# A transformer layer in split fp32: twelve instead of eight projection pairs by seven half products, with other step times and longer reckoned transfers

## The chip, the cores and the metric

One NeuronCore of one Trainium2 chip runs one launch of the whole layer. The metric is the device time of the launch in microseconds, median over runs. The engines of the core are PE (matrix products), DVE (VectorE), ACT (ScalarE), POOL (GpSimd) and SP, which here only issues transfers.

## What is computed

One encoder layer on x of 512 tokens by 1024 channels, all in float32 (DFF = 2816):

```
proj = h @ w_in                       # q, k, v of both mixers: 3840 columns
qa, ka, va, qb, kb, vb = split(proj)  # rope_partial on the first 16 of 64 channels of each head's q and k
o_a = windowed_gqa_sink(qa, ka, va, sink)   # 16 heads, 4 kv heads, |i-j| <= 128
o_b = dilated_mixture(qb, kb, vb)           # 3 groups of 4 heads, strides 1, 4, 16
gates = sigmoid(h @ w_gate + b_gate)        # 2 x 1024
mixed = g_a * (o_a @ w_br_a) + g_b * (o_b @ w_br_b)
h = layer_norm(ALPHA * h + mixed @ w_out)
f = (silu(h @ w_ff_gate) * (h @ w_ff_up)) @ w_ff_down
h = layer_norm(ALPHA * h + f)
```

## The kernel before

**Split fp32.** Each fp32 operand is kept as a high part (rounded to the type `fp32r`) and a rest. A product is three matmuls: high by high, high by rest, rest by high. The high part is a copy, on ACT as a rule and on DVE where that is free; the rest is a subtraction on DVE. Splitting the weights is most of the work of both engines.

**Units and pairs.** The weights lie in units of 128 output columns by 1024 rows, as two halves of 512 rows (128 partitions by 512 columns, 256 KB each). A plain unit (`feat_x`) loads two halves, splits both, and runs 8 row blocks x 3 matmuls over all 512 tokens: 24 matmuls of 512 columns. `pair_x(ua, ub)` does two units at once as a two by two block product (two units by two row halves, times two row halves by two token halves) with seven instead of eight half products: the weight blocks are A11, A12, A22 and the sums S1 = A21 + A22, S3 = A11 + A21, S2 = S1 + A11 and S4 = A12 + S2 (up to the signs), the x blocks are B11, B21, B22 and T1 to T4, which the step X (`x_forms`) makes once from x. Each half product is 4 x 3 matmuls over 256 columns, 84 for the pair. `fetch` loads A11, A12, A22 and the first part of S1 and S3 on SP; the second part of S1 and S3 is a transfer on POOL that adds into the block already there (`load_sum`). `form` makes S2 and S4 with one DVE addition each, `sep` splits the seven blocks (the copy on ACT, the subtraction at L399 before), and two DVE operations and four ACT copies put the result together.

**Rotation.** q and k of a plain unit are rotated out of PSUM in `rotate`: four DVE operations over 128 partitions, one of them a stream shuffle that swaps the rotated halves. Tiles that lie in SBUF are rotated together in `turn_rows`: their few rotated rows (16 of each 64) are brought by small transfers on SP into one tile G, shuffled into H, multiplied, added, and brought back. `q_post`, `k_post` then move halves with further SP transfers (L811).

**What sets the order.** Nothing runs in the order of the text. Every `op(...)` is recorded with the engines that can do it, a cost, the tiles it reads and writes and a priority: the time `pr.T` that PE's recorded work has reached, plus an offset (weight work lies 130 us ahead, `LOOK`). `Program.run` then plans the whole kernel: at each moment every free engine takes the ready operation of the lowest priority whose buffers fit the limits (`ws` for blocks as loaded, `whl` for split ones, `gen` for the rest). The outcome is a fixed order on each engine, and on the chip each engine runs its own in that order, waiting for semaphores. For transfers, the planner reckons a landing time from rates and constants (`LATE`, 2.4 or 3.2 us and so on). The words of `ORDER` are the steps that are recorded, in turn:

```
for w in ORDER.split():
    step(w)
```

`VA`, `V0`, `V12` are values; `q1`, `k1`, `Q10`, `K10` and so on are q and k units; `P:a,b` is a pair of units; `g` is a gate unit (its number counts up by itself); `R` turns the tiles gathered since the last R; `A0` to `A3` are the attention of mixer A by key head, four query blocks each, `B0` to `B3` mixer B by head slot; `O` fetches a block of A's output; `L` sets limits. After them come the branch products, the output product, the first norm, and the feed-forward stage, which also uses seven half products, and the second norm.

Of the kernel before, what the change touches and what calls it, by code (L numbers as in the profile page):

```python
# [15 lines left out]
P = 128  # L16
# [36 lines left out]
SPARE, SPARE2 = 12, 12  # L53
# [10 lines left out]
LATE = 2.4  # L64
OAP = (-88.0, -88.0, -88.0, -88.0)
# [29 lines left out]
BY_DMA = ()  # L95
AWAY = range(8, 16)
N_WSA, N_WHLA = 8, 16
# [36 lines left out]
class Program:  # L134
# [67 lines left out]
    def run(self):  # L202
# [26 lines left out]
        while n_left:  # L229
# [11 lines left out]
            while progress:  # L241
                progress = False
                for e in engines:
# [27 lines left out]
                    if e == SP:  # L271
                        end = now + (0.62 if 14 < now < SLOW else 0.47)
                        moved = max(moved, now + 0.9) + (1.5 if now < 9.5 else RATE if 90 < now < 165 else RATE2 if 285 < now < 325 else 1.0 if now < SLOW else 0.92) * cost
                        o.done = moved + (LATE if 95 < now < 150 else 2.4 if 14 < now < SLOW else 0.87)
                    elif o.moves:
                        end = now + cost
                        moved = max(moved, end + 0.3) + (1.0 if 14 < now < SLOW else 0.92) * o.moves
                        o.done = moved + (0.87 if e == ACT else 6.2 if ACC < now < 420 else 3.2 if 14 < now < SLOW else 2.2)
                    else:
                        end = now + cost  # L280
                        o.done = end
# [50 lines left out]
def hybrid_layer(ctx: ExitStack, tc: tile.TileContext, wpack, xT, xtok, sink, bgate,  # L332
# [10 lines left out]
                  "unit": UNITS, "oa": N_OA, "st": 4, "x4": 4, "wf": N_WF})  # L343
# [250 lines left out]
    def pair_x(ua, ub):  # L594
# [12 lines left out]
        def form(key, of, x, y):  # L607
            tt(lambda: W[of].t, lambda: W[x].t, lambda: W[y].t, ALU.add, [W[x], W[y]], [W[of]], S, -LOOK)
# [93 lines left out]
    def turn_rows(tiles):  # L702
# [6 lines left out]
        for i, R in enumerate(tiles):  # L709
# [5 lines left out]
        op([(DVE, dve(S, extra=0.03))], lambda e: nc.vector.stream_shuffle(h_(), g(), SHUF2), reads=gs, writes=[H], prio=EV)  # L715
# [3 lines left out]
           reads=[H, *[(s_, i) for i in range(4)]], writes=[H], prio=EV)  # L719
# [156 lines left out]
    def turned_values(u, nt, turn_by=0, done=None):  # L876
# [3 lines left out]
        for i in range(2):  # L880
            ps = done
# [18 lines left out]
        for b in range(NR):  # L900
# [6 lines left out]
            op([(PE, 0.18)], turn, reads=[*src, ident], writes=[pb])  # L907
# [46 lines left out]


# [11 lines left out]
    def turned_probs(srcs, toks):  # L967
# [7 lines left out]
        op([(PE, 0.36)], go, reads=[*toks, ident], writes=[pb])  # L975
# [6 lines left out]
    def turned_pairs(srcs, toks):  # L982
# [7 lines left out]
        op([(PE, 0.36)], go, reads=[*toks, ident], writes=[pb])  # L990
# [60 lines left out]
    def unit_b(hs, q, k, v0, v1, v2):  # L1051
# [99 lines left out]
        dil = []  # L1151
        for half in range(2):
# [5 lines left out]
            def pv(e, half=half, xs=xs, od=od):  # L1158
# [7 lines left out]
                y for vs in (v1, v2) for t in vs[2 * half:2 * half + 2] for y in vtok(t)], writes=[od])  # L1166
            t = slot(F32, "att")
            dil.append(t)
            part = lambda od=od: od.t.rearrange("p (r i a) -> p r a i", r=2, a=2)
# [32 lines left out]
        t = slot(F32, "att")  # L1202
        op(cp_alts(S, True), lambda e: copy(e, t.t[0:64], o.t[64:128]), reads=[o], writes=[t])
        a = 64 * (hs % 2)
# [27 lines left out]
    def gate(f, ps=None):  # L1232
        if ps is None:
# [6 lines left out]
           reads=[ps, bg], writes=[t], prio=EV)  # L1240

# [25 lines left out]
    ka = k_near(psk, 4)  # L1267
    qa = q_near(psq, 4, (0, 0))
# [43 lines left out]
    def units_of(w):  # L1312
# [8 lines left out]
        if w[0] == "q":  # L1321
            return U_QA + i, lambda t: qa.extend(q_post(t, 4, ((i // 2) % 2,) * 2))
        if w[0] == "k":
            return U_KA + i, lambda t: ka.extend(k_post(t, 4))
# [4 lines left out]
    def step(w):  # L1329
# [4 lines left out]
        elif w[:2] == "P:":  # L1334
            both = [units_of(x) for x in w[2:].split(",")]
            for (u, f), t in zip(both, pair_x(*[u for u, _ in both])):
# [7 lines left out]
        elif w == "R":  # L1344
            tiles = [t for t, _ in env["turn"]]
            turn_rows(tiles)
# [8 lines left out]
        elif w[0] == "q":  # L1355
            i = int(w[1])
            kv = (i // 2) % 2
            qa.extend(dense_q(U_QA + i, 4, (kv, kv)))
        elif w == "k1":
            ka.extend(dense_k(U_KA + 1, 4))  # L1360
        elif w[0] == "A":
            g = int(w[1])
            for b in range(NR):
                unit_a(g, b, qa[4 * g:4 * g + 4], ka[g], env["va"])
# [4 lines left out]
        elif w[0] in "QK":  # L1369
            pair, g = int(w[1]), int(w[2])  # L1370
            u, f = units_of(w)
            env["turn"].append((in_sbuf(u), f))
        elif w == "V0":
            env["v0"] = turned_values(U_V0, 8, 1)
        elif w == "V12":
# [9 lines left out]
    for w in ORDER.split():  # L1385
# [660 lines left out]
```

## Time and profile before

| what | value |
|---|---|
| median of 3 runs | 727.95 us (727.42 to 728.01) |
| span of the profiled execution, first to last instruction | 725.8 us |
| median run less that span | 2.15 us |
| instructions | 14412 |
| bytes moved by DMA | 140.30 MB, mean 193 GB/s |
| PE, DVE, ACT, POOL busy | 99%, 90%, 65%, 18% of the span |
| mean granted clock of PE | 0.996 |

The profile is of one execution. It gives that execution's span and no time of the whole launch; the timed runs, which are launches, lie 1.6 to 2.2 us above the span. Busy shares of PE overstate its work, since matmuls are pipelined; the list of waits and the distance between starts say more. In a row of waits, "A <- B: 1.2, 1, 1.2" reads: A's engine stood idle before A until B ended, 1.2 us in total, once, 1.2 us at most.

### The profile page before, as it was taken

The page shows a single profiled execution, that of the slowest core. Times are in us where ns is not written, and L with a number is a line of the kernel's source. Part 1 is how long each engine was busy: PE and PEld are TensorE (multiplying, and loading weights), DVE is VectorE, ACT ScalarE, POOL GpSimd, SP SyncE. Part 2 cuts the span into 40 slices and gives each one's busy share as a digit, 9 for nine tenths or more (in the row PEclk, how much of TensorE's full clock was granted, in tenths as well). Part 3 has the DMA queues.
Part 4 walks back from the last instruction along what each step waited for, and adds up shares of the span by engine and source line. Part 5 has one row for each costly group of instructions (what it writes and reads, how often), then busy time and mean ns, then how long its engine had stood idle before and what let it go on. Part 6 is the DMA issues. An engine that isn't in the chain of part 4 may idle for free.

```text
span 725.8 us, 14412 instructions
## 1 busy us (share of the span) xinstructions
PE 717.3 (99%) x4767; PEld 666.2 (92%) x4767; DVE 655.6 (90%) x1408; ACT 471.4 (65%) x1077; POOL 134.0 (18%) x297
## 2 busy tenths in 40 slices
PE   9999999999999999999999999999999999999995
PEld 7889999989988888988888999999999999999985
DVE  6999999889997898898967898899999999899987
ACT  5757798868778665666534666756666566666821
POOL 0021211111100731450020021111112211212000
PEclk9999999999999999999999999999999999999998
DMA  8978788856577689965681499676888888979302
GB/s 256 309 155 202 191 213 246 211 135 172 170 192 185 160 228 253 309 217 185 216 209 44 116 267 228 154 199 155 200 254 212 193 215 225 258 184 200 97 30 87
DMA packets 88010, 140.30 MB, mean 193 GB/s; under 512 B 11136, under 2 KB 24064, under 8 KB 87936
## 3 DMA queue, kind: packets, MB, share of 16 engines
q1 hardware_dynamic: 74336, 114.87, 51.7%
q0 software_dynamic: 13328, 24.39, 20.5%
q8 instruction: 37, 0.61, 0.3%
q14 instruction: 37, 0.30, 0.1%
q10 hardware_dynamic: 272, 0.13, 0.1%
HBM read 114.97 MB, written 7.60 MB: 169 GB/s over the span
## 4 chain that ended last, share of the span: by engine, by line
PE 99%; DVE 1%; DVEq 0%; issue 0%
PE ps L1692 10%; PE ps L1691 9%; PE ps L1690 9%; PE ps L523 9%; PE ps L524 9%; PE ps L525 9%; PE ps L1901 4%; PE ps L1903 4%; PE ps L1902 4%; PE ps L641 3%; PE ps L640 3%; PE ps L639 3%; PE ps L973 3%; PE ps L1480 3%; PE ps L1481 3%; PE ps L1482 3%
## 5 line engine op out<-in xcount | busy, mean ns | idle before, releaser
L373 ACT ACTIVATE sl<-sl 128x512 fp32r<-128x512 f32 (+3 forms) x419 | 230.8, 583 | 59.7 <-DVE sl L544 31.1
L544 DVE TENSOR_TENSOR sl<-sl,sl 128x512 fp32r<-128x512 f32 (+3 forms) x378 | 222.4, 621 | 5.1 <-ACT sl L373 3.4
L373 ACT ACTIVATE sl<-ps 128x256 f32<-128x256 f32 (+5 forms) x209 | 88.7, 445 | 91.6 <-PE ps L1692 56.8
L387 POOL DMA_DIRECT2D sl<-wpack x60 | 53.1, 885 | 342.9 <-DMA sl<-wpack 118.2
L1691 PE MATMUL ps<-sl,sl 128*128 128x256 f32 x352 | 96.8, 275 | 0.0
L1692 PE MATMUL ps<-sl,sl 128*128 128x256 f32 x352 | 96.8, 275 | 0.0
L1690 PE MATMUL ps<-sl,sl 128*128 128x256 f32 x352 | 96.8, 275 | 0.0
L523 PE MATMUL ps<-x,sl 128*128 128x512 f32 (+1 forms) x241 | 93.9, 389 | 0.0
L525 PE MATMUL ps<-x,sl 128*128 128x512 f32 (+1 forms) x241 | 91.4, 379 | 0.0
L524 PE MATMUL ps<-x,sl 128*128 128x512 f32 (+1 forms) x209 | 79.5, 380 | 0.0
L1690 PE MATMUL ps<-x,sl 128*128 128x256 f32 x264 | 72.6, 275 | 0.0
L1691 PE MATMUL ps<-x,sl 128*128 128x256 f32 x264 | 72.6, 275 | 0.0
L1692 PE MATMUL ps<-x,sl 128*128 128x256 f32 x264 | 72.6, 275 | 0.0
L1691 PEld LDWEIGHTS ps<-sl,sl 128*128 128x128 f32 x352 | 67.6, 192 | 0.1
L1690 PEld LDWEIGHTS ps<-sl,sl 128*128 128x128 f32 x352 | 67.6, 192 | 0.1
L1692 PEld LDWEIGHTS ps<-sl,sl 128*128 128x128 f32 x352 | 67.6, 192 | 0.0
L399 DVE TENSOR_TENSOR sl<-sl,sl 128x512 fp32r<-128x512 f32 x94 | 62.8, 682 | 1.8 <-ACT sl L373 1.3
L525 PEld LDWEIGHTS ps<-x,sl 128*128 128x128 f32 x241 | 45.9, 190 | 6.5
L1690 PEld LDWEIGHTS ps<-x,sl 128*128 128x128 f32 x264 | 50.6, 192 | 0.4
L1691 PEld LDWEIGHTS ps<-x,sl 128*128 128x128 f32 x264 | 50.6, 192 | 0.4
L523 PEld LDWEIGHTS ps<-x,sl 128*128 128x128 f32 x241 | 46.0, 191 | 5.4 <-ACT sl L373 0.3
L1692 PEld LDWEIGHTS ps<-x,sl 128*128 128x128 f32 x264 | 50.7, 192 | 0.0
(172 smaller groups left out, 1851.0 us busy)
## 6 DMA issues: line engine op xcount, KB each, us to landing
sl<-wpack SPq DMA_DIRECT2D x249, 256.0 KB, 3.9
sl<-wpack POOLq DMA_DIRECT2D x60, 256.0 KB, 5.3
sl<-sl SPq DMA_DIRECT2D x110, 128.0 KB, 3.1
wf<-wpack SPq DMA_DIRECT2D x51, 256.0 KB, 5.2
wf<-wpack POOLq DMA_DIRECT2D x24, 256.0 KB, 6.2
oa<-sl SPq DMA_DIRECT2D x32, 128.0 KB, 3.6
sl<-sl SPq DMA_DIRECT2D x68, 32.0 KB, 2.6
sl<-oa SPq DMA_DIRECT2D x8, 256.0 KB, 5.1
```

The lines of the kernel that those rows point to most:

```text
L373: nc.scalar.activation(dst, src, AF.Copy)
L387: op([(POOL, 1.0)], lambda e: nc.gpsimd.dma_start(b.t, src2, accum_op=ALU.add), reads=[b], writes=[b], prio=prio, moves=1.65)
L399: op([(DVE, dve(S))], lambda e: nc.vector.tensor_tensor(l.t, src.t, f32(h.t), op=ALU.subtract), reads=[src, h], writes=[l], prio=prio, abs ...
L523: mm(o, a, x0, start=(k == 0 and begins), stop=False, skip_group_check=split)
L524: mm(o, a, x1, start=False, stop=False, skip_group_check=split)
L525: mm(o, b, x0, start=False, stop=(k == nk - 1), skip_group_check=split)
L544: op([(DVE, dve(w))], lambda e: nc.vector.tensor_tensor(dst(), x(), y(), op=o), reads=reads, writes=writes, prio=prio)
L1690: mm(o, wh, pairs(bh[k]()), start=(first and k == 0), stop=False, skip_group_check=True)
L1691: mm(o, wh, pairs(bl[k]()), start=False, stop=False, skip_group_check=True)
L1692: mm(o, wl, pairs(bh[k]()), start=False, stop=(k == 3), skip_group_check=True)
L1901: mm(ps.t, x0, pairs(w[0].t), start=(first and m == 0), stop=False, skip_group_check=True)
L1902: mm(ps.t, x0, pairs(w[1].t), start=False, stop=False, skip_group_check=True)
```

## The change

The table of steps is new. Twelve pairs stand in it instead of eight (the words P and D), and single gates are spread between the last attention steps instead of eight at the end. A number behind `@` shifts the priority of everything that the step records by so many us (negative: earlier). `D:` is a pair whose S2 and S4 are made by transfers on POOL that add one SBUF block into another, and `r` is a turn whose shuffle is made by eight-row transfers on SP instead of a DVE shuffle.

```diff
-VA q1 A0 q2 q3 g X P:k1,q4 R A1 P:q5,g P:q6,q7 R A2 P:g,g A3 P:g,g L P:Q00,K00 R V12 P:Q01,K01 R P:Q02,K02 R V0 B0 Q10 K10 R Q11 K11 R B1 O O Q12 K12 R O O B2 B3 O O O O g8
+q1@-471 X@-159 VA A0@-92 q2@-21 P:q3,g@-28 R@-36 D:k1,q4@-16 R@89 P:q5,Q01@-152 D:q6,q7@-32 r@680 D:g,g P:g,Q00@-10 L P:g,K00@-42 A1@-39
+R@180 V12@-5 P:g,K01@-30 R@22 P:Q02,K02@-15 R@-10 A2@-71 A3@-67 V0@36 P:K10,Q10@-17 B0@-44 O@-1217 O@-237 R@-587 K11@-20 B1@-33 P:Q12,Q11@-22
...
-SPARE, SPARE2 = 12, 12
+SPARE, SPARE2 = (10, 12)
+LONG = 1.3
-FORMS = -60.0
-VAL = -100.0
-OA_AFTER = (0, 0, 0, 0, 0, 0, 0, 0)
+FORMS = -165.0
+VAL = -130.0
+OA_AFTER = (0, 0, 0, 0, 0, 1, 1, 0)
-N_WSA, N_WHLA = 8, 16
+N_WSA, N_WHLA = (8, 18)
...
 (Program.run: the reckoned landing of SP's and of other transfers)
-                        o.done = moved + (LATE if 95 < now < 150 else 2.4 if 14 < now < SLOW else 0.87)
+                        o.done = moved + (LONG if now < 380 else 1.0) * (LATE if 95 < now < 150 else 2.4 if 14 < now < SLOW else 0.87)
...
 (pair_x, form)
+            if by_dma:
+                a, b = W[of], W[x if y == of else y]
+                op([(POOL, 1.0)], lambda e: nc.gpsimd.dma_start(a.t, b.t, accum_op=ALU.add), reads=[a, b], writes=[a],
+                   prio=-LOOK, moves=1.65)
+                W[key] = a
+                return
...
 (turn_rows)
+        if by_dma:
+            hs_ = []
+            for i, R in enumerate(tiles):
+                for h in range(2):
+                    for z in range(2):
+                        hs_.append((H, 4 * i + 2 * h + z))
+                        op([(SP, 0.1)], lambda e, R=R, i=i, h=h, z=z: nc.sync.dma_start(
+                            H.t[32 * i + 16 * h + 8 * z:32 * i + 16 * h + 8 * z + 8], R.t[64 * h + 8 - 8 * z:64 * h + 16 - 8 * z]),
+                           reads=[(R, 1), (R, 2)], writes=[hs_[-1]], prio=EV)
+        else:
+            op([(DVE, dve(S, extra=0.03))], lambda e: nc.vector.stream_shuffle(h_(), g(), SHUF2), reads=gs, writes=[H], prio=EV)
...
 (gate: plain gates of branch B are stored to DRAM and read back later, as those of pairs were)
+        if f in AWAY:
+            put_away(f)
...
 (the planner's costs of transposes on PE)
-        op([(PE, 0.36)], go, reads=[*toks, ident], writes=[pb])
+        op([(PE, 0.436)], go, reads=[*toks, ident], writes=[pb])
...
 (steps)
+        w, _, later = w.partition("@")
+        pr.T += float(later or 0)
         step(w)
+        pr.T -= float(later or 0)
```

The new file also holds code that no word of the table reaches (values by half products, values out of a pair, mixture sums by transfers); q and k tiles are now kept by their unit's number instead of being appended, since units no longer come in sequence. Line numbers are higher by some 4 to 200: a pair's matmuls, L639 to L641 before, are L649 to L651 after; its split at L399 is L403; the DVE helper L544 is L548; the load L381 is L385 and the addition on POOL L387 is L391.

Over the whole program, by the built order: matmuls over 512 columns 1711 before and 1519 after, over 256 columns 2672 and 3008; full tensor operations on DVE 633 and 651, half ones with a scalar 71 and 75, casts of 512 columns 24 and 13, half casts (two shapes of 256 columns) 1 and 8, shuffles 13 and 11; POOL transfers 93 and 107; SP transfers of 256 KB 342 and 352, of 16 rows 72 and 76, of 8 rows 0 and 20.

PE, behind the first five units and one plain unit (names: `ps` is a PSUM tile, `x` holds x split, `sl` a split weight or values). Before, another plain unit (ps116) and, in its middle, the transposes of the values of A:

```order
L525 MATMUL ps116_519<-x47_94,sl80_394 128x512
L905 MATMUL ps121_550<-ident_65,sl99_450 128x128
L905 MATMUL ps121_550<-ident_65,sl119_535 128x128
L905 MATMUL ps122_553<-ident_65,sl99_450 128x128
L905 MATMUL ps122_553<-ident_65,sl119_535 128x128
L523 MATMUL ps116_519<-x442_242,sl82_402 128x512
```

After, behind the same five units and one plain unit (ps94), the first pair begins (256 columns, first product A11 by B11):

```order
L527 MATMUL ps94_451<-x444_245,sl67_336 128x512
L528 MATMUL ps94_451<-x446_253,sl67_336 128x512
L529 MATMUL ps94_451<-x444_245,sl68_337 128x512
L649 MATMUL ps109_509<-x48_98,sl70_345 128x256
L650 MATMUL ps109_509<-x412_105,sl70_345 128x256
L651 MATMUL ps109_509<-x48_98,sl71_346 128x256
```

A plain unit and the values' transposes have moved behind the pair.

POOL, from the first blocks of attention A0 on (COPY is the sink's column for the softmax of one head; L387, L391 add a loaded block; L614 adds one SBUF block into another). Before:

```order
L1020 COPY sl144_627<-nsink_66 128x1
L1020 COPY sl145_630<-nsink_66 128x1
L387 DMA sl152_663<-wpack 128x512
L387 DMA sl173_747<-wpack 128x512
L387 DMA sl201_881<-wpack 128x512
L387 DMA sl211_953<-wpack 128x512
L1020 COPY sl243_1086<-nsink_66 128x1
```

After:

```order
L1198 COPY sl182_858<-nsink_66 128x1
L614 DMA sl138_659<-sl145_685 128x512
L391 DMA sl174_830<-wpack 128x512
L614 DMA sl153_727<-sl161_756 128x512
L1198 COPY sl206_975<-nsink_66 128x1
L1198 COPY sl207_979<-nsink_66 128x1
L1198 COPY sl208_981<-nsink_66 128x1
L614 DMA sl146_688<-sl138_659 128x512
L1198 COPY sl213_996<-nsink_66 128x1
L614 DMA sl164_773<-sl153_727 128x512
```

The S2 and S4 additions of two D pairs (sl138 into sl146, sl153 into sl164) now stand between the copies of A0's second block.

SP, around the first packed turn of more than one tile (L381, L385 load a block; L712, L722 bring rows into G; L732 brings eight rows into H; L1046 stores attention output). Before:

```order
L381 DMA sl211_953<-wpack 128x512
L712 DMA sl214_959<-sl195_835 16x512 x2
L381 DMA sl222_993<-wpack 128x512
L712 DMA sl214_959<-sl206_907 16x512 x2
L381 DMA sl234_1063<-wpack 128x512
L1046 DMA oa236_1071<-sl235_1066 64x4x128
```

After:

```order
L722 DMA sl142_678<-sl128_611 16x512
L385 DMA sl161_756<-wpack 128x512
L722 DMA sl142_678<-sl128_611 16x512
L385 DMA sl164_773<-wpack 128x512
L732 DMA sl169_786<-sl115_532 8x512 x4
L732 DMA sl169_786<-sl128_611 8x512 x2
L385 DMA sl174_830<-wpack 128x512
L732 DMA sl169_786<-sl128_611 8x512 x2
```

The rows for G and H of two tiles now stand among the block loads of the two D pairs (sl161, sl164, sl174).

More of the change, by code (lines that the diff above doesn't have):

```diff
@@ L277, in run @@
                         moved = max(moved, end + 0.3) + (1.0 if 14 < now < SLOW else 0.92) * o.moves
-                        o.done = moved + (0.87 if e == ACT else 6.2 if ACC < now < 420 else 3.2 if 14 < now < SLOW else 2.2)
+                        o.done = moved + (LONG if now < 380 else 1.0) * (0.87 if e == ACT else 6.2 if ACC < now < 420 else 3.2 if 14 < now < SLOW else 2.2)
                     else:
@@ L873, in scores, with turned_values @@
         return go, [(qt, "h"), (qt, "l"), (kt, "h"), (kt, "d"), (kl, "h"), (kl, "d")]
-    def turned_values(u, nt, turn_by=0, done=None):
+    def turned_values(u, nt, turn_by=0, done=None, made=None):
         src = []
@@ L1151, in unit_b @@
         dil = []
+        add_up = hs in SUM_BY_DMA
+        E = [slot(F32, "att"), slot(F32, "att")] if add_up else []
         for half in range(2):
```

203 lines of the change are left out of this document (182 added, 21 removed).

## The prediction

> **What bounds the kernel now.** I read the busy shares first, then who waited for whom, then the busy time by stretch, then the end of the chain that ended last, and last single rows for the price of each instruction.
>
> ```profile
> PE 717.3 (99%) x4767; PEld 666.2 (92%) x4767; DVE 655.6 (90%) x1408; ACT 471.4 (65%) x1077; POOL 134.0 (18%) x297
> ```
>
> The list of waits on PE over the whole run has one entry:
>
> ```profile
> PE ps L459 <- DVE eps L510: 1.2, 1, 1.2
> ```
>
> So the matrix engine waits 1.2 us at the start and then never again. The same by stretch (columns: PE busy, weight loads, DVE, ACT, POOL, granted clock, DMA share, GB/s), and the first and last row of the chain at its end:
>
> ```profile
> 0.00:340.00 340.00, 338.81 (x2109) 309.56 (x2110) 304.43 (x751) 247.60 (x603) 75.09 (x229) 1.00 0.77 210
> 340.00:420.00 80.00, 80.00 (x431) 71.19 (x430) 67.67 (x116) 41.51 (x83) 7.76 (x9) 1.00 0.56 150
> 420.00:700.00 280.00, 280.00 (x2147) 269.57 (x2147) 264.28 (x509) 178.65 (x385) 51.17 (x59) 1.00 0.78 195
> ```
> ```profile
> 718.26 0.23 PE ps L1482
> ...
> 722.15 0.40 DVE sl L1543
> ```
>
> PE is busy for all of 340:700 at full clock, and for all but 1.2 us before. A share of "busy" alone would prove little, since matmuls overlap; but with no wait in the list and one matmul's start on the heels of the next (rows below), PE's own work sets the end at 718.5, and 7.3 us of vector work and store follow. A time saved must therefore come out of PE's sum, and a loss must come as a wait on PE that does not exist today. The second engine is DVE: 304.4 of 340 in the stretch that the change touches, and early on nearly all of it:
>
> ```profile
> 20.00:60.00 40.00, 40.00 (x195) 35.11 (x194) 39.46 (x82) 23.98 (x47) 6.33 (x12) 1.00 0.80 220
> 60.00:110.00 50.00, 50.00 (x428) 49.36 (x427) 47.78 (x104) 44.11 (x106) 10.21 (x18) 1.00 0.81 203
> ```
>
> **The change, PE.** Four more pairs are done by seven half products. Two plain units are 2 x 8 x 3 = 48 matmuls over 512 columns; a pair is 7 x 4 x 3 = 84 over 256. By the built order the counts go from 1711 to 1519 (512 columns) and from 2672 to 3008 (256); transposes and everything else on PE keep their counts, so the change does what it says. The price of one is the distance between starts, not the "mean ns" of a group, which contains the pipeline. Of 28 rows over 512 columns, and of 110 rows over 256, the first and the last:
>
> ```profile
> 46.15 0.38 PE L524 MATMUL ps<-x,sl 128*128 128x512 f32 x1
> ...
> 51.98 0.38 PE L524 MATMUL ps<-x,sl 128*128 128x512 f32 x1
> ```
> ```profile
> 419.81 0.28 PE L1691 MATMUL ps<-x,sl 128*128 128x256 f32 x1
> ...
> 431.98 0.28 PE L1692 MATMUL ps<-sl,sl 128*128 128x256 f32 x1
> ```
>
> (51.98 - 46.15) / 27 = 0.2159 us and (431.98 - 419.81) / 109 = 0.1117 us. The change removes 192 x 0.2159 = 41.45 and adds 336 x 0.1117 = 37.53: PE's work falls by 3.92 us, 0.98 per pair.
>
> The Trainium skill, page "TensorE: Matmul & The Clock Gate", section "Wait — 56ns, not 53.3ns?", puts the step at columns / 2.4 GHz plus about 2.5 ns. It fits the long matmuls here (0.2158 against 0.2159) and not the short ones (0.1092 against 0.1117); by it the saving would be 192 x 0.2158 - 336 x 0.1092 = 4.74 us, an estimate from that page. The measured step decides, so I keep 3.92.
>
> **DVE and ACT.** A plain unit needs two splits into a high part (ACT) and a rest (DVE); a pair needs seven, two sums that form S2 and S4, and two sums at the end. Prices, again by distance of starts where rows follow each other:
>
> ```profile
> 28.31 3.69 DVE L399 TENSOR_TENSOR sl<-sl,sl 128x512 fp32r<-128x512 f32 x6
> 24.15 0.42 DVE L570 SCALAR_TENSOR_TENSOR sl<-sl 128x256 f32<-128x256 f32 x1
> 24.49 0.41 DVE L544 TENSOR_TENSOR sl<-sl,sl 128x256 f32<-128x256 f32 x1
> L375 DVE CAST sl<-sl 128x512 fp32r<-128x512 f32 x14 | 5.8, 420 | 0.7 <-DMA sl<-sl 0.6
> L375 DVE CAST sl<-sl 128x256 fp32r<-128x256 f32 x1 | 0.3, 294 | 0.0
> L715 DVE STREAM_SHUFFLE sl<-sl 64x512 f32<-64x512 f32 x7 | 5.1, 732 | 0.0
> ```
>
> Six in 3.69 us is 0.60 each (3.69 less one tail of 0.08), the half size 0.34, a cast 0.34 and half a cast 0.21 (less the same 0.08), a shuffle 0.65. Counts by the order: +18 full tensor operations (24 for the four pairs, less 6 that the D pairs give to DMA), +4 half ones, -11 casts, +7 half casts, -2 shuffles: 10.8 + 1.4 - 3.7 + 1.5 - 1.3 = +8.7 us. In 0:340, which becomes some 336, DVE then has 313 us of work: 93% against 90%. ACT gains 18 full and 18 half activations, at most
>
> ```profile
> L373 ACT ACTIVATE sl<-sl 128x512 fp32r<-128x512 f32 x337 | 200.7, 622 | 51.9 <-DVE sl L544 30.0 <-DVE sl L747 7.2 <-DVE sl L570 2.7
> L647 ACT ACTIVATE sl<-ps 128x256 f32<-128x256 f32 x32 | 12.0, 375 | 3.7 <-PE ps L641 3.6
> ```
>
> 18 x 0.62 + 18 x 0.38 = 18 us on 248 of 340: no limit. On the path that sets the end I cost DVE and ACT at nothing, since PE's stream covers them; the cover is thin before 110 us, where DVE has 0.54 + 2.22 = 2.76 us free of 90. That is the first rival.
>
> **Transfers.** Each pair loads five blocks on SP and adds two on POOL where two units load four on SP; the three D pairs put two more additions each on POOL, from SBUF to SBUF. That is +14 on POOL. SP gains 34 rows: 4 blocks, 3 gates stored and 3 read back, 20 pieces of 16 KB that replace two shuffles, 4 small turn pieces.
>
> ```profile
> sl<-wpack SPq DMA_DIRECT2D x249, 256.0 KB, 3.9
> sl<-wpack POOLq DMA_DIRECT2D x60, 256.0 KB, 5.3
> sl<-sl SPq DMA_DIRECT2D x110, 128.0 KB, 3.1
> sl<-sl SPq DMA_DIRECT2D x68, 32.0 KB, 2.6
> sl<-oa POOLq DMA_DIRECT2D x8, 256.0 KB, 7.5
> q1 hardware_dynamic: 74336, 114.87, 51.7%
> q0 software_dynamic: 13328, 24.39, 20.5%
> 82.41 1.20 SPq L723 DMA_DIRECT2D sl<-sl  x2
> ```
>
> By queue, POOL's 24.39 MB take 0.84% of the span per MB and SP's 0.45%: 14 x 0.26 MB and 10 x 0.26 MB add about 3.1% + 1.2% of 726 us, 31 us, which over the first 340 lifts the share from 0.77 to about 0.86. There is room. SP's queue gets 34 x 0.6 = 20 us more of issue; what stands behind the small pieces there are weight blocks for products that PE reaches later. An addition from SBUF to SBUF is not in this trace: from below 3.1 us (SBUF to SBUF, half the size, on SP), from above 7.5 (POOL, addition of a block just written); I take 5.3, the row of the same size, queue and operation. It lies beside PE's other work unless the chain in the second rival comes late; bounds on the path: 0 to what is priced there. Not a gain, since nothing waits for the DVE sums today.
>
> **Order.** The first pair now starts right after the first plain unit, the first scores of attention later; the longer reckoned transfers move users of a block later or its load earlier and add no instruction. The feed-forward stage keeps its instructions. Where a place in the order costs PE nothing before, I found none in the new order that must cost: the gaps that the softmax leaves between scores and their transposes, and between transposes and the product with the values, are filled with about as many matmuls as before.
>
> **Sum.** 3.92 us less on PE, nothing added on the path. The profiled span of 725.8 would be 721.9; the median run lies 2.15 above the span (727.95), which is launch and end and stays. Forecast: 727.95 - 3.92 = 724.0.
>
> **Rivals.**
> First, DVE binds early. By the order, PE has done 1.8 pairs where it had just begun its first (57 us of PE work), and 5.1 instead of 4.0 at 107. A pair costs DVE 10 x 0.60 + 0.34 = 6.3 us against 2.4 for two plain units, 3.9 more (2.7 for a D pair). At 107 that is 2.7 to 4.3 us more work against 2.76 us free: up to 1.5 us late; at 57, 1.8 x 2.7 to 3.9 = 4.9 to 7.0, less 2.4 for the four operations of a rotation that moves into the packed turn, against 0.54 free: up to 4.1 late if nothing of it could be done ahead. Against it: attention work that filled DVE there now comes later. In the middle some 2.3 us of waits: 726.3.
>
> Second, the other side: the chain of a D pair. S1 is loaded (3.9), added to (5.3), added into A11 for S2 and that into A12 for S4 (5.3 to 7.5 each): 19.8 to 24.2 us before S4 can be split, where DVE's sums give 3.9 + 5.3 + 1.2 = 10.4. PE eats a pair in 84 x 0.1117 = 9.4. On POOL the addition for S4 stands behind the one for S2 and ahead of copies that the softmax needs, so a late one holds both. If a D pair is late by 1.3 us three times over, the saving is gone; from 1.8 us each it is slower by over 0.2% (3 x 1.8 - 3.92 = +1.5); at 3 us each 727.95 - 3.92 + 9 = 733.0. For it: POOL stops at an addition until the load before it has landed,
>
> ```profile
> POOL sl L387 <- DMA sl<-wpack: 43.7, 6, 32.8
> ```
>
> six times in 20:340; without the idle start (32.8) five times 2.2 us. Against it: PE was held up by none of these, and D products come a pair or more behind their loads in the order.
>
> The Trainium skill, page "TensorE: Matmul & The Clock Gate", section "HAM oscillation — how this bites in real kernels", adds that PE idle for over about 3.4 us comes back at half clock. No stretch here shows it before the end (1.00 throughout), as PE never idles; it would make a long wait dearer by up to about 1.7 us, an estimate from that page's window.
>
> Third, the short matmuls run closer to that page's step than in the row above: 723.2. Little speaks for it, all rows give 0.1117.
>
> **Numbers.** 0.2% of 728 us, 1.46 us, is about what a measurement here can tell from no change. Forecast, PE stays full within a microsecond: 0.63. DVE early (726.3, half of it within 0.2% of before): 0.22. D chain: 0.08, nearly all slower. Short step: 0.03. Other small waits: 0.04, mostly with part of the gain left. Faster 0.80, same 0.13, slower 0.07. Range: 723.2 (the third rival) to 727.4 (the first rival beyond its middle).
>
> **What would show it.** Right: PE's list of waits still has only the entry at the start, PE ends near 714.5, 336 more short and 192 fewer long matmuls at the same steps, DVE near 664 us busy, DMA share in 0:340 near 0.86, the tail 7.3 us. Wrong: a wait of PE on DVE's splits between 35 and 110 us (first rival), or on splits behind the POOL additions with SBUF source between 60 and 150 (second), or a clock under 1.00 after one of them.

## The result, and the profile after

| kernel | median | runs | ratio to before (95% interval) |
|---|---|---|---|
| before | 727.98 us | 727.42 to 728.41 (4) | 1 |
| after | 734.82 us | 733.65 to 737.8 (4) | 1.0099 (1.0074 to 1.0124) |

Forecast were 724.0 us in a range of 723.2 to 727.4, and a slower kernel at 0.07. The change costs 1%; the forecast missed by 10.8 us. Disturbed runs are left out below, one of four of the first e1 and two of four in e11, which e16 repeats.

The busy shares after, first line of the page:

```profile
PE 717.6 (98%) x4911; PEld 668.4 (91%) x4911; DVE 663.0 (91%) x1418; ACT 483.8 (66%) x1109; POOL 150.6 (21%) x311
```

PE has 144 matmuls more, as counted, and DVE 663 us, near the 664 that were forecast. But the profiled span is 732.2 us instead of 725.8, and the list of waits on PE (total, times, longest) is no longer one entry:

```profile
PE ps L1342 <- DVE sl L1176: 3.1, 1, 3.1
PE ps L1218 <- DVE sl L1156: 1.5, 2, 1.2
PE ps L463 <- DVE eps L514: 1.2, 1, 1.2
PE ps L527 <- ACT sl L377: 0.8, 1, 0.8
PE ps L649 <- ACT sl L657: 0.5, 1, 0.5
```

5.9 us of waits are new. Delays too short for the list count as well. I added up over all rows of PE how much farther the next start lies than the price of the row (0.2159 us for 512 columns, 0.1117 for 256, for other shapes their median distance before). After has 10.4 us more of this than before: 0.8 at 80 to 100, 2.1 at 140 to 160, 0.7 at 260 to 280, 6.0 at 280 to 300, 0.4 behind 400, the rest in small amounts. The spans say the same: 732.2 - 725.8 + 3.9 of saved work = 10.3.

To compare kernels below, I call loss what the median lies above before's median on the same chip, plus the 3.9 us of work that twelve pairs save (nothing for eight): 10.8 us for after (734.82 - 727.98 + 3.92).

The stretches of the prediction, after (PE, weight loads, DVE, ACT, POOL, clock, DMA share, GB/s):

```profile
0.00:340.00 340.00, 332.78 (x2224) 306.43 (x2225) 306.52 (x752) 258.07 (x630) 91.35 (x243) 0.99 0.84 225
340.00:420.00 80.00, 79.83 (x402) 70.07 (x401) 66.08 (x113) 40.69 (x81) 6.99 (x8) 1.00 0.58 161
420.00:700.00 280.00, 280.00 (x2176) 270.38 (x2175) 265.92 (x512) 180.58 (x390) 52.30 (x60) 1.00 0.78 199
```

Nearly all that PE loses lies ahead of 340. The same view in finer stretches, before and then after:

```profile
260.00:280.00 20.00, 20.00 (x117) 18.10 (x116) 17.28 (x44) 13.56 (x30) 3.47 (x4) 1.00 0.92 214
280.00:300.00 20.00, 20.00 (x110) 17.83 (x109) 17.27 (x49) 9.71 (x27) 4.07 (x8) 1.00 1.02 288
```
```profile
260.00:280.00 20.00, 19.89 (x125) 17.76 (x124) 18.41 (x55) 15.69 (x42) 9.67 (x36) 1.00 0.83 208
280.00:300.00 20.00, 16.10 (x89) 13.80 (x88) 14.61 (x42) 14.21 (x38) 8.35 (x24) 0.93 1.00 293
```

At 280:300 PE and DVE lose busy time, while the DMA share is at 1.00. It was at 1.02 before, too, and PE did not wait. (A share can pass 1, so it counts packets that overlap, and 1.00 alone does not prove that the engines are full.) What SP issues there after (start, length, line, count; L877 and L832 are moves of 128 KB inside SBUF, L385 loads of weight blocks):

```profile
265.57 7.27 SPq L877 DMA_DIRECT2D sl<-sl  x8
272.95 5.02 SPq L832 DMA_DIRECT2D sl<-sl  x8
278.07 5.22 SPq L877 DMA_DIRECT2D sl<-sl  x8
...
283.97 1.85 SPq L385 DMA_DIRECT2D sl<-wpack  x4
...
289.34 4.89 SPq L385 DMA_DIRECT2D sl<-wpack  x6
```

For 18 us SP issues no weight block, then many. But before had such pauses too, 16 us up to 278.48 and 12 us up to 294.09 (L856 are moves, L381 loads):

```profile
266.46 8.87 SPq L856 DMA_DIRECT2D sl<-sl  x8
...
278.48 1.77 SPq L381 DMA_DIRECT2D sl<-wpack  x4
...
294.09 5.91 SPq L381 DMA_DIRECT2D sl<-wpack  x9
```

What differs is whether somebody stands waiting for the blocks. ACT's waits for weight blocks in 20:340, before and then after:

```profile
ACT sl L373 <- DMA sl<-wpack: 0.7, 1, 0.7
```
```profile
ACT sl L377 <- DMA sl<-wpack: 8.4, 6, 2.8
```

In after, 5.1 of the 8.4 us lie in 280:298. DVE waits there for ACT's copies; below it, the chain up to PE's wait:

```profile
DVE sl L403 <- ACT sl L377: 3.6, 2, 2.5
```
```profile
286.88 6.96 DMA sl<-wpack
...
293.86 0.03 ACT sl L377
...
295.55 0.28 ACT sl L377
...
295.86 0.42 DVE sl L379
296.28 0.34 DVE sl L1176
```

A block on its way for 6.96 us holds ACT's copy up to 293.86. ACT runs its list in order, and the copies of the turned probabilities (295.55) stand behind that one; DVE makes the rest of these (L1176), and PE waits 3.1 us for it. The wait of 1.2 us that ends at 155.35 has the same form: a move of 128 KB, on its way for 5.76 us, holds DVE (L825), and the split that PE needs (L1156) stands behind it. Then PE comes back at half clock, seen in the distance of its starts:

```profile
293.26 0.38 PE L529 MATMUL ps<-x,sl 128*128 128x512 f32 x1
296.76 1.85 PE L1342 MATMUL ps<-sl,sl 128*128 128x256 f32 x8 [3.12 <-DVE sl L1176]
298.40 0.63 PE L527 MATMUL ps<-x,sl 128*128 128x512 f32 x1
298.83 0.63 PE L528 MATMUL ps<-x,sl 128*128 128x512 f32 x1
...
300.52 0.38 PE L529 MATMUL ps<-x,sl 128*128 128x512 f32 x1
300.74 0.38 PE L527 MATMUL ps<-x,sl 128*128 128x512 f32 x1
```

0.43 us from start to start up to 300.5, then 0.22. The record of the granted clock has 0.5 for 3.41 us there: 1.7 us more, which are part of the 6.0.

### The profile page after: what moved, and what is told of

It is laid out like the page before. It is cut to its first block, busy times and chain, and to the rows that moved or that the text cites. A ratio compares the mean times of both kernels' runs of the same rounds, so it can differ in the third digit from the quotient of the medians.

```text
span 732.2 us, 14826 instructions
## 1 busy us (share of the span) xinstructions
PE 717.6 (98%) x4911; PEld 668.4 (91%) x4911; DVE 663.0 (91%) x1418; ACT 483.8 (66%) x1109; POOL 150.6 (21%) x311
## 4 chain that ended last, share of the span: by engine, by line
PE 89%; DVE 4%; DMA 3%; SPq 1%; issue 1%; ACT 1%; DVEq 0%
PE ps L1895 9%; PE ps L1896 9%; PE ps L1894 9%; PE ps L527 6%; PE ps L528 6%; PE ps L529 6%; PE ps L649 4%; PE ps L650 4%; PE ps L651 4%; PE ps L2105 4%; PE ps L2106 4%; PE ps L2107 4%; PE ps L1686 3%; PE ps L1684 3%; PE ps L1685 3%; PE ps L1151 2%
## 5 line engine op out<-in xcount | busy, mean ns | idle before, releaser
L377 ACT ACTIVATE sl<-sl 128x512 fp32r<-128x512 f32 (+3 forms) x437 | 242.0, 586 | 69.9 <-DVE sl L548 41.6
L548 DVE TENSOR_TENSOR sl<-sl,sl 128x512 fp32r<-128x512 f32 (+3 forms) x408 | 240.4, 626 | 2.5 <-ACT sl L377 1.6
L391 POOL DMA_DIRECT2D sl<-wpack x68 | 59.9, 881 | 357.8 <-DMA sl<-wpack 161.5
L377 ACT ACTIVATE sl<-ps 128x256 f32<-128x256 f32 (+5 forms) x206 | 85.7, 438 | 70.8 <-PE ps L1896 52.9
L1895 PE MATMUL ps<-sl,sl 128*128 128x256 f32 x352 | 96.8, 275 | 0.0
L1896 PE MATMUL ps<-sl,sl 128*128 128x256 f32 x352 | 96.8, 275 | 0.0
L1894 PE MATMUL ps<-sl,sl 128*128 128x256 f32 x352 | 96.8, 275 | 0.0
L527 PE MATMUL ps<-x,sl 128*128 128x512 f32 (+1 forms) x177 | 69.5, 393 | 0.8 <-ACT sl L377 0.8
L529 PE MATMUL ps<-x,sl 128*128 128x512 f32 (+1 forms) x177 | 67.5, 382 | 0.0
L403 DVE TENSOR_TENSOR sl<-sl,sl 128x512 fp32r<-128x512 f32 x78 | 52.5, 682 | 5.2 <-ACT sl L377 4.0
L528 PE MATMUL ps<-x,sl 128*128 128x512 f32 (+1 forms) x145 | 55.6, 384 | 0.0
L548 DVE TENSOR_TENSOR sl<-sl,ps 128x512 f32<-128x512 f32 (+1 forms) x71 | 46.5, 659 | 8.2 <-PE ps L2107 5.4
L649 PE MATMUL ps<-sl,sl 128*128 128x256 f32 x192 | 53.5, 278 | 0.0
L650 PE MATMUL ps<-sl,sl 128*128 128x256 f32 x192 | 52.8, 275 | 0.0
L651 PE MATMUL ps<-sl,sl 128*128 128x256 f32 x192 | 52.8, 275 | 0.0
L1895 PEld LDWEIGHTS ps<-x,sl 128*128 128x128 f32 x264 | 50.6, 192 | 0.4
```

The lines of the kernel that those rows point to most:

```text
L377: nc.scalar.activation(dst, src, AF.Copy)
L391: op([(POOL, 1.0)], lambda e: nc.gpsimd.dma_start(b.t, src2, accum_op=ALU.add), reads=[b], writes=[b], prio=prio, moves=1.65)
L527: mm(o, a, x0, start=(k == 0 and begins), stop=False, skip_group_check=split)
L528: mm(o, a, x1, start=False, stop=False, skip_group_check=split)
L529: mm(o, b, x0, start=False, stop=(k == nk - 1), skip_group_check=split)
L548: op([(DVE, dve(w))], lambda e: nc.vector.tensor_tensor(dst(), x(), y(), op=o), reads=reads, writes=writes, prio=prio)
```

## The experiments

Eighteen runs; "after" in them means the changed kernel. Unless said, its planned order is kept on every engine, so that only the edit differs; e6 and e10 to e16 are planned anew.

**First idea: SP's queue (theory 1).** SP was to be relieved of moves, on POOL's queue instead.

```diff
-op([(SP, 0.4)], lambda e, t=t, z=z, a=a, d=d: nc.sync.dma_start(     # k_pairs, L877
+op([(SP, 0.4)], lambda e, t=t, z=z, a=a, d=d: nc.gpsimd.dma_start(
```

> Changed kernel, same planned order, but the moves of L877 (k_pairs, 128 KB each) are issued by POOL's queue instead of SP's; bytes, tiles and users are the same. Theory 1 (SP issues its transfers one after the other, 0.62 to 0.9 us each, and the weight loads behind 26 small moves at 265.5 to 284.0 come too late): sixteen of these 26 leave the queue, the loads at 284 to 288 are issued some 10 us earlier, the wait PE ps L1342 <- DVE sl L1176 of 3.1 us and the slow clock behind it go, about 5 to 6 us: 728 to 730 us. Theory 2 (the additions of the D pairs on POOL) and theory 3 (the 8-row pieces of the turned rows): no change, 734 to 736. Theory 5 (the DMA engines are full there, share 1.00, and the landing is late whoever issues): no change, 734 to 736. If POOL is late instead, its additions are (5.7 us each): then slower than 736.

Measured 736.32 us, ratio 1.0105 (1.0087 to 1.0123): no gain. The chain up to PE's wait:

```profile
282.43 12.49 DMA sl<-wpack
...
297.37 0.34 DVE sl L1176
```

SP issued the four blocks from 278.55 instead of 283.97 on, and the block that the chain hangs on at 282.43 instead of 286.88. Yet it was 12.49 us on its way, and PE waited 3.2 us at the same place. With L832 moved as well:

> As e1_pairs_pool, and the moves of L832 (q_post, k_post) are issued by POOL too: 110 moves of 128 KB leave SP's queue, about 70 us of its issue. Theory 1: the loss at 80 to 100, 140 to 160 and 260 to 300 goes (9 to 10 us), less what comes back because POOL issues a move later than SP did: 725 to 729 us. Theory 5 (full DMA engines): 734 to 736. Theories 2 and 3: 734 to 736.

736.9 us, 1.0115 (1.0081 to 1.0149). Here the edit brings a wait of its own: POOL's additions and its small softmax copies now stand in one list with moves (`272.45 9.87 DMA sl<-oa` in the chain), so the run does not tell the theories apart. In the first one the landing of the block does. The Trainium skill, page "DMA: Bandwidth & Descriptors", section "Issuing engines are not separate DMA queues", says that transfers of all issuing engines share the same 16 DMA engines, and that another issuer saves only the time of issuing. The 12.49 us agree.

**The two new forms of the change (theories 2 and 3).**

```diff
-nc.gpsimd.dma_start(a.t, b.t, accum_op=ALU.add)          # form, D pairs
+nc.vector.tensor_tensor(a.t, a.t, b.t, op=ALU.add)
```

> Changed kernel, same planned order, but the six additions from tile to tile of the D pairs (POOL, 256 KB, 5.7 us each) are done by VectorE (six adds of 128x512, about 0.62 us each, 3.7 us of VectorE). Theory 2 (the chain of transfers of the D pairs delays their products): 728 to 731 us. Theory 1 (SP's queue): these additions stand on POOL, SP is as before, so 734 to 737, the larger value where VectorE's 3.7 us more stand in the stretch in which PE waits for it. Theory 5: 1.5 MB less of moving at 60 to 260, but none at 260 to 300: at most 1 us gain.

735.47 us, 1.0097 (1.008 to 1.0115), the same wait, 4.3 us long: the additions of the D pairs are not the cause.

```diff
-nc.sync.dma_start(H.t[... 8 rows ...], R.t[...])   # 20 of them, L732
+nc.vector.stream_shuffle(h_(), g(), SHUF2)          # at the place of the last of each turn
```

> Changed kernel, same planned order, but the 20 transfers of 8 rows (L732) are left away and VectorE's shuffle (two, 0.6 us each) does their work as it did before. Theory 3 (these pieces fill SP's queue before the load at 260, and before the one at about 135): the losses near 254 to 264 and after go, up to 6 us, 728 to 731. Theory 1 with the moves as the main load of the queue: SP gains 16 x 0.65 = 10 us near one turn and 4 x 0.65 = 2.6 us near the other (which lies at 254 to 264), so the weight loads at 284 come 2.6 us earlier: 731 to 733. Theories 2 and 5: 734 to 736.

735.51 us, 1.0103 (1.0081 to 1.0124). The wait at 297 shrank to 1.3 us, and others of 2.0 us (at 153) and 1.9 us (at 265) came up. Not the cause either; a loss that is taken away in one place comes back in another.

**Order on SP, or bytes (theory 1 against 5).** Twelve of the 26 moves belong to heads that PE scores only after 298 us. In e4 they go behind the next five blocks:

```diff
-o.fn(e)
+if e == SP and any(abs(now - t) < 0.05 for t in WAITING): self.kept.append(o.fn)
+else:
+    if e == SP and now > BEHIND: (issue what is kept)
+    o.fn(e)
```

> Changed kernel with one edit: the twelve moves (L877, L832) for heads that PE scores only after 298 us, which stand on SP's queue between 265 and 284, are issued behind the next weight loads instead (the five loads that went out at 283.7 to 286.1). PE, VectorE, ScalarE, POOL, all bytes and all other places stay. Theory 1 (order on SP's queue): the loads go out some 5 to 7 us earlier, at 277 to 280, the wait of 3.1 us PE ps L1342 <- DVE sl L1176, that of 0.8 us before it and the slow clock behind them go: 728 to 731 us. Theory 5 (the DMA engines could not land these blocks earlier whatever the order): PE still waits over 2 us between 282 and 298, 733 to 736. Theories 2 and 3 (D pairs, 8-row pieces): 734 to 736. Theory 6 (VectorE is late by its own work): 734 to 736.

735.98 us, 1.0114 (1.0099 to 1.0129). SP's rows there (L394 is the load, L886 and L841 the moves):

```profile
276.18 1.82 SPq L394 DMA_DIRECT2D sl<-wpack  x4
...
279.05 3.12 SPq L886 DMA_DIRECT2D sl<-sl  x4
...
285.57 3.82 SPq L886 DMA_DIRECT2D sl<-sl  x4
289.50 1.61 SPq L394 DMA_DIRECT2D sl<-wpack  x1
```
```profile
289.50 5.08 DMA sl<-wpack
```
```profile
PE ps L1351 <- DVE sl L1185: 5.4, 1, 5.4
```

Five blocks did go out 8 us earlier, and PE's wait of 0.8 us at 287 went. But the sixth, on which the large wait hangs, now stood behind the twelve moves, which took up to 1 us each, and PE waited 5.4 us for it at the same matmul. So the edit held back the very block that matters, and the time alone does not decide between the theories. The landings say more: this block, the sixth behind the pause in SP's list, was issued at 282.43 in e1, at 286.88 in after and at 289.50 in e4, and it landed at 294.9, 293.8 and 294.6. Within these 7 us the time of issue hardly moves the landing. Theory 1, that a late issue on SP makes this block late, falls. In e5 the second fetches of mixer A's output are left out:

```diff
-lambda e: nc.gpsimd.dma_start(st.t, src(1), accum_op=ALU.add)   # L1505, 8 x 256 KB
+lambda e: None
```

> Changed kernel, same planned order, but the eight second fetches of the first attention's output (L1505, POOL, 256 KB each, added to what is there) are left out, so the result lacks one of its two parts: 2 MB less on the DMA engines between 262 and 310. Issues on SP as before. Theory 5 (full engines: landing 5 to 8.7 us for the loads issued at 284 to 292): landing falls to 3 to 5 us and the waits of ScalarE for wpack (5.1 us in all) mostly go: 729 to 731. Theory 1 (the loads are issued late, at 283.7): they still are, and gain only what their landing gains before PE's wait, 1 to 2 us: 732 to 734. Theories 2, 3 and 6: 734 to 736.

730.18 us (ten runs, 728.49 to 735.16), 1.0047 (1.0026 to 1.0067): 4.6 us faster than after, as theory 5 expected. The profiled execution (735.16) is the slowest of the ten and no faster than after's, so it does not show where the gain lies; its wait at L1342 is 2.1 us instead of 3.1, and another has come up:

```profile
PE ps L1342 <- DVE sl L1176: 2.1, 1, 2.1
PE ps L1151 <- DVE sl L1141: 1.3, 1, 1.3
```

So these fetches cost 4.6 us in this stretch. The edit takes two things away at once, 2 MB on the DMA engines and the wait of their users for a second landing. A planner that only knows SP as slower:

```diff
-end = now + (0.62 if 14 < now < SLOW else 0.47)
+end = now + (0.70 if 255 < now < 300 else 0.62 if 14 < now < SLOW else 0.47)
```

> Changed kernel, but the planner reckons 0.70 us instead of 0.62 for an issue on SP between 255 and 300 of its time (the records show 0.62 to 0.9 there); all engines' order up to 255 is the same, behind it planned anew. Theory 1: the plan knows that the loads come late and puts other work ahead: the waits at 282 to 298 shrink to under 1.5 us, 729 to 732. Theory 5: a plan that only knows SP better doesn't know the full engines: 733 to 737. Theories 2, 3 and 6: 733 to 737.

740.82 us, 1.0172 (1.0149 to 1.0194), outside all expectations: a worse order, most of its waits spread over 285 to 337 us. By the planner's own reckoning this order already leaves gaps of 9.3 us on PE, 8.1 more than after's, so it says nothing on the theories. And the kernel itself:

> The changed kernel once more beside the others on this chip: 733 to 737 us by every theory; it shows how far its own runs scatter (before, 733.65 to 737.8).

734.75 us, 1.0095 (1.0079 to 1.0112).

**The mirror: 2 MB more.** Behind each second fetch a transfer that nobody waits for, in both kernels:

```diff
+nc.gpsimd.dma_start(extra, wpack[k, :, 0:S])     # HBM to HBM, 256 KB, eight times
```

> Kernel before, same planned order, with eight extra transfers of 256 KB from HBM to HBM that nobody waits for, one behind each second fetch (POOL, at 261 to 300): 2 MB more on the DMA engines. Theory 5 (the engines' time there is what the loads wait for, in before too; their share is 0.92 and 1.02 in 260 to 300): loads land later and PE starts to wait, 730 to 734 us. Rival (before has room there, and the loss of the changed kernel is its order alone): 727.5 to 729.

> Changed kernel, same planned order, with the same eight extra transfers of 256 KB (2 MB) at 262 to 310. Theory 5: the mirror of the run without the second fetches (4.6 us faster): 737.5 to 742 us. Rival (the order alone, engines not the limit): 734 to 736.

Before: 730.09 us, 1.0041 (1.0025 to 1.0058), 2.7 us slower than it was, as theory 5 expected. After: 737.14 us, 1.0137 (1.0116 to 1.0157), 2.4 slower, just under theory 5's 737.5. Load on the DMA engines there costs both kernels about the same (the extra transfers also take time and places in POOL's queue, which these runs don't separate); before has no room left either. So the load explains how a wait comes about, not why before has none.

**A plan with better prices.** I fitted what a transfer takes on the engines to the issue and landing times in the records of before, after and e4: 0.62 us for a move of 128 KB, 0.17 for a small piece, 0.75 for 256 KB from HBM, 1.4 for an addition, and 1.6 us of way behind it; the mean error of one landing is 0.7 us. These prices are estimates. The planner reckons 0.40, 0.10, 0.73 and 1.65.

```diff
+MOVE, LAND = {0.4: 0.62, 0.1: 0.17}, 2.22
-o.done = moved + (LONG if now < 380 else 1.0) * (LATE if 95 < now < 150 else 2.4 ...)
+o.done = moved + (LAND if 14 < now < SLOW else 0.87)
 (and new offsets in ORDER)
```

> Changed kernel whose planner reckons transfers as the records of both kernels show them, in the stretch up to 340 us: 0.62 us of the DMA engines for a move of 128 KB (instead of 0.40), 0.17 for the small pieces of turned rows (0.10), 0.75 for 256 KB (0.73, up to 1.4 times that in places), 1.4 for an addition of 256 KB, a landing 2.2 us behind (2.4 to 3.1), 0.50 or 0.63 us for an issue on SP (0.62); no factor LONG. The offsets of the steps are fitted anew to it (22 of them differ by 1 to 90). Pairs, forms, instructions and bytes are the same. Theory 5 (the plan put more into the engines than they could carry, because it reckoned the moves too cheap): PE's waits fall from 10 us to under 4, 724 to 728 us. Theory 6 (VectorE at 91% is late by its own work): 732 to 736. Rival (a planned order never holds on the chip to better than 10 us): 732 to 738.

> A second order from the same reckoning as e10_reckoned_a, with offsets of its own: the same expectations, 724 to 728 us by theory 5 and 732 to 738 by the others; how far the two lie apart shows what an order's luck is worth.

748.16 and 745.03 us, 1.0265 (1.0223 to 1.0308) and 1.0237 (1.0209 to 1.0264): far worse than any expectation, with waits all over (the first order's):

```profile
PE ps L1217 <- DVE sl L1155: 4.2, 3, 3.5
PE ps L526 <- ACT sl L376: 3.0, 1, 3.0
```

Both plans leave PE gaps of 1.5 us, nearly as few as after's 1.2, and lose 24.7 and 21.6 us on the chip. So the fitted prices with little reserve behind them made worse orders than the old prices with LONG. With 2 us of reserve in each landing (`LAND` = 3.62, an issue at 0.55 or 0.64 us, new offsets) the same prices gave

> The changed kernel's twelve pairs, planned as in e10_reckoned_a (0.62 us of the engines for a move of 128 KB), but with a landing of 3.6 us instead of 2.2 behind it, so 2 us of reserve, and 0.55 or 0.64 us for an issue. The runs e10 lost 27 us in waits on PE with next to no reserve. If the reserve is what an order lives by: under 6 us of waits, 726 to 731 us. If twelve pairs leave too little room whatever the plan says: 733 to 740.

734.31 us, 1.0088 (1.0063 to 1.0112), a loss of 9.7 us: 12 to 15 less than without the reserve, and still no gain. The time lies where the expectation puts it if twelve pairs leave too little room whatever the plan says.

**The pairs or the order?** Four of the twelve pairs undone, and the rest planned anew from the changed order's steps (five offsets differ slightly):

```diff
-P:g,K01@-30 ... P:K10,Q10@-17 ... P:Q12,Q11@-22 ... P:g,g@-18
+K01@-30 g   ... K10@-17 Q10   ... Q12@-22 Q11   ... g@-18 g
```

> Changed kernel with four of its twelve pairs undone (K10 with Q10, Q12 with Q11, g with K01, and one g with g), so eight as before; the changed order of the rest, the factor LONG, the D pairs and the r turns stay, planned by the same reckoning (three offsets differ slightly so that the plan has no gap). PE has 4 x 0.98 = 3.9 us more work than the changed kernel. Theory 5a (the pairs' own transfers and VectorE work are the load that the stretch from 225 to 300 could not carry): PE's waits fall from 10 us to 3 or less, 729 to 733 us, no slower than the changed kernel in spite of its work. Theory 5b (the order and the reckoning are what fails, the number of pairs is not): the waits stay, 737 to 741 us.

742.07 and 738.69 us. Once more:

> The same kernel as e11_four_pairs_less (four pairs undone in the changed order), of which only two runs were undisturbed (738.7 and 742.1 us). Theory 5b: 737 to 742 again, with waits of PE of 8 us or more behind the start. Theory 5a (the added pairs' load): 729 to 733, with waits under 3 us.

740.91 us, 1.0184 (1.0165 to 1.0204), and its profile:

```profile
PE 722.5 (98%) x4767; PEld 667.0 (90%) x4767; DVE 652.1 (88%) x1394; ACT 473.9 (64%) x1082; POOL 137.5 (19%) x303
```
```profile
PE ps L1216 <- DVE sl L1154: 2.9, 4, 2.0
PE ps L1215 <- DVE sl L377: 1.6, 1, 1.6
PE ps L461 <- DVE eps L512: 1.2, 1, 1.2
PE ps L1383 <- DVE sl L950: 1.2, 3, 0.7
```

With as many pairs as before (x4767) and less for DVE, this order loses 13.0 us, the largest part (6.2) at 120 to 160. The kernel with four pairs more is 6.1 us faster (734.82 against 740.91), of which 3.9 is their work. So an order of eight pairs can lose as much as one of twelve; the number of pairs is not needed for it. Two more orders, one of before's pairs with LONG and offsets fitted anew, one of the twelve pairs from another start:

> Kernel before, its eight pairs and bytes, with the reckoned landings longer by LONG = 1.3 up to 380 us and the offsets of its steps fitted anew (the plan has no gap). Theory 5a: the bytes and their stretch are as before, 727 to 731 us. Theory 5b (an order planned with longer landings, or any newly fitted order, holds worse): 732 to 738 us.

> The changed kernel's pairs, forms and reckoning, unchanged, with the offsets of its steps fitted once more from another start: another order whose plan ends at the same time within 0.3 us. Theory 5a or 5b alike: as the changed kernel, 731 to 739; under 729 would mean that this one order was unlucky.

732.42 us, 1.0051 (1.0033 to 1.0068), and 736.92 us, 1.0119 (1.0085 to 1.0152); losses of 3.9 and 12.3 us, though the plans leave PE gaps of only 0.6 and 1.5 us. The last one: twelve pairs, prices as in e10, SP's issue as the records have it (0.66 us for a move or a piece, 0.71 for a store, 0.50 for a load), the reserve of e13, and offsets chosen for an order that bears late transfers.

> The changed kernel's twelve pairs in another order: transfers reckoned as in e10, an issue on SP at 0.66 us for a move or a small piece, 0.71 for a store and 0.50 for a load (as the records show them), 2 us of reserve in each landing, and the offsets chosen so that the order loses least when issues and landings come late by random amounts (0.05 and 0.8 us in the mean). Theory 5b (what fails in the changed kernel is an order without room for late transfers; the pairs themselves are worth their 3.9 us): PE's waits under 5 us beyond those at the start, 724 to 729 us. Rival (twelve pairs load VectorE, SP's queue and the DMA engines too far for any order): 731 to 738 us.

732.23 us, 1.0058 (1.004 to 1.0077): the best of the orders of the twelve pairs, 2.6 us better than after. It lies in the rival's range (731 to 738) and not in that of theory 5b. Its largest waits:

```profile
PE ps L463 <- DVE eps L514: 1.2, 1, 1.2
PE ps L1765 <- DVE sl L1747: 0.8, 1, 0.8
PE ps L1385 <- DVE st L1310: 0.5, 1, 0.5
```

The waits in the list are 4.0 us in all, of which 1.2 stood before, too; by its span this execution loses 6.5 us (728.4 - 725.8 + 3.9), so most of the loss lies in delays too short for the list. No version beat before.

## Why the prediction was wrong, point by point

- **PE's work: right.** The steps are those of before. Of 8 rows over 512 columns up to 293.26 us, the distance is 0.2157; of 113 rows over 256 columns,

```profile
421.61 0.28 PE L1895 MATMUL ps<-x,sl 128*128 128x256 f32 x1
...
434.11 0.28 PE L1896 MATMUL ps<-sl,sl 128*128 128x256 f32 x1
```

  12.50 / 112 = 0.1116. The 3.92 us are there, and the third rival (short step) is not.
- **DVE and the first rival: right in size, and not the cause.** 663.0 us against 664. (Of the rival's "2.7 to 4.3 us more work" at 107, the first should be 3.0: 1.1 pairs at 2.7.) Between 35 and 110 us PE waits once, 0.5 us, on ACT.
- **The D chain: right.** The addition inside SBUF took 5.7 us (5.3 was taken), no wait of PE leads to it (the additions lie at 60 to 115 us), and e2 without it is no faster:

```profile
sl<-sl POOLq DMA_DIRECT2D x6, 256.0 KB, 5.7
```

- **DMA: the mean was right (0.84 against 0.86), "There is room" was wrong.** I read one row over 340 us. In stretches of 20 us, before stood at 0.92 and 1.02 between 260 and 300 already; in e5, e8 and e9, transfers of 2 MB there move either kernel by 2.4 to 4.6 us.
- **SP's queue, costed at nothing.** I wrote that weight blocks for later products stand behind the small pieces. Blocks that PE needs soon do stand behind moves there. But issuing them earlier (e1) won nothing: the block that PE waits for landed at the same time within 1.1 us, whether issued at 282, 287 or 289. That the load on the DMA engines sets this time is the likeliest reason, but argued.
- **The step that failed: "Order", and with it "nothing added on the path".** I wrote that I found no place in the new order that must cost, having compared how many matmuls fill each gap. That answers whether PE has work, not whether the work's operands arrive. The term that I put at nothing measured 10.3 us on PE in the profile: weight blocks and moves land late, ACT and DVE stand before them in their fixed lists, and PE waits for what stands behind. By the medians, eight pairs in the changed order lose 13.0 us (e16), other orders of the twelve pairs 8.3 to 24.7 (e15, e10_reckoned_a), and a new order of before's own pairs 3.9 (e12).
- **The chances.** All of my rivals were edits inside the kernel; "the order as a whole fits the chip worse" had no line and no price, though the table was new from end to end. That is where the 0.07 for slower was too low.
- **The clock.** The Trainium skill, page "TensorE: Matmul & The Clock Gate", section "HAM oscillation — how this bites in real kernels", was drawn on for up to 1.7 us behind a long wait. The trace agrees on the size: 3.41 us at 0.5. It differs on what sets it off: 3.1 us of waiting sufficed here and 2.0 us in e3, where the section's rule is over about 3.4.

What stays open: which of the some fifty offsets and steps of the new table makes the order bad. The experiments undid four of its pairs, its D and r forms, its order on one queue and its reckoning, and none of these is it alone. Nor is it excluded that twelve pairs make any order harder: both orders with reserve (e13, e15) came out where that rival put them. The two plans themselves differ in one thing that no run tests. Between 20 and 340 us, the middle one of all transfers has 9.4 us between its reckoned landing and its first planned user in before (381 transfers), and 4.2 us in after (426). LONG, which sets the reckoned landings some 0.7 to 1 us later, explains a small part of that. Nor is it the whole answer: in e10_reckoned_a, which reckons earlier landings, it is 7.3 us, and that order loses more.

## What to carry to other kernels

A list of waits with one entry says that this order works, not that there is room: add a known load to the kernel before (here 2 MB, 2.7 us) and see. A change that plans a full kernel anew is a new order first and an edit second; give "the new order loses some per cent" a line and a chance of its own, and look at each stretch where the old one is at its limit. Where an order is planned ahead and each engine runs its list as written, plan reserve into the landings, not only fitted prices: the order with reserve (e13) lost 12 to 15 us less than the two without (e10), though all three also differ in their offsets.

## What the runs showed of the hardware

- Waits of PE of 2.0 us (e3), 2.6 us (e9, e14) and 3.1 us (after) were followed by 3.41 us at half clock, one of 5.4 us (e4) by 6.83 us; waits of 2.1 us (e5) and 2.4 us (e9) by none. So a wait of 3 us costs nearly 5 us (after), or 6.7 us where 6.83 us at half clock follow (e7, 3.3 us).
- Blocks issued over a span of 7 us landed at the same time within 1.1 us (e1, after, e4, the same weight block): issuing earlier brought it no sooner.
- By the fit above, an estimate that no single row shows, a move of 128 KB over 64 partitions holds the DMA engines 0.62 us, nearly as long as a load of 256 KB over 128 (0.75).
- On SP, after, up to 340 us, a move of 128 KB is issued 0.64 us after one of its kind, a piece of 32 KB 0.63 and a load of 256 KB 0.61 (medians of 86, 44 and 62 pairs of rows): bytes do not set its pace.
